# Float32r and bfloat16 products grouped within each accumulation of a two-layer decoder trunk

## The chip, the cores and the metric

The kernel runs on one core of one Trainium2 chip. The metric is the device time of one execution in microseconds. Three timed runs of the kernel before gave 1263.82, 1265.33 and 1266.68 us; the median is 1265.33.

## What is computed

A trunk of two layers over 1024 tokens of width 1024, with 256 memory tokens, everything in float32 (`x`, `mem` and all weights):

```python
for layer in range(2):
    h = x @ w_in[layer]                         # 1024 -> 3072: main | mem q | main gate | mem gate
    if layer == 0:  y_main = causal_pool(u_main)        # windows 2, 4, 8, 16 by group of 256 channels, then a 256 x 256 map
    else:           y_main = forgetting_attention(u_main, k, v, cum)   # 16 heads of 64, causal
    y_mem = memory_attention(q_mem, mem, w_mem_kv[layer])              # 4 heads of 128
    y = concat(y_main * silu(g_main), y_mem * silu(g_mem)) @ w_out[layer]      # 1536 -> 1024
    x = layer_norm(sqrt(2) * x + y)
# ahead of layer 1: k, v, forget logits = x @ w_kv_shared; cum = cumsum(log_sigmoid(logits))
# forgetting attention: softmax(q.k / 8 + cum[t] - cum[s]) @ v
```

## The kernel before

**Precision by three products.** Each float32 operand is split in two: `hi` is its float32r rounding, and a pair `lo` of bfloat16 tiles holds `lo[0]`, the remainder, and `lo[1]`, the operand itself in bfloat16. `three(a, b)` (line 184) gives for one contraction tile of 128 the three products that are summed in a PSUM bank: large `(ah, bh)` in float32r, and two small ones in bfloat16:

```python
return (ah, bh), (al[1], bl[0]), (al[0], bl[1])
```

The trace shows float32r operands as f32. The first operand is the stationary one, loaded ahead of each product by a load instruction (PEld in the profile); the second streams, mostly 512 columns. `hi_lo` (line 155) makes the split: ScalarE the `hi` (line 158), VectorE `lo[0]` (159), GpSimd `lo[1]` (160). In the forgetting attention `gp_hi_lo` (162) does all three on GpSimd for weights (163 to 165). Weights come through `split_w` (167): one DMA of 128 x 512 to a `raw` buffer (four of them), then `hi` and the `lo` pair in one buffer each of the tag `w` (six).

**Slabs.** Most of the work on TensorE is done in slabs (`slab`, line 194): 128 output channels for all 1024 tokens. A slab has two weight pieces of four contraction tiles. It allocates two PSUM banks (tag `pj`, three banks), one for each 512 tokens, and goes: for each piece, for each half of the tokens, for each of four contraction tiles, the three products (line 205), 48 in all. After the last product of a half, `evac` empties its bank: for gates a tanh on ScalarE (line 218) and a product on VectorE (219), else copies. A slab is a generator that yields after each product.

**Other sums.** `project` in `mem_kv` (line 231) sums 24 products of 256 columns for keys and values of the memory; `mm3` (189) sums a list of products, for the map of pooled channels (line 556), the logits and values of the memory attention (317, 342) and of the forgetting attention (756, 803), all seen at line 192; `v_first` (620) makes the first values and the forget logits with 272 columns (line 635); `OutProj.products` (403) does the output projection by chunks (`c`) of 512 of the 1536 inputs and 256 tokens, four banks, three chunks in turn 2, 0, 1 (line 411). After the third chunk `norm` (450) empties the banks on VectorE (459, 460), normalizes (462 to 472) and stores; in layer 0 TensorE then transposes the result (281) for layer 1.

**Order.** In layer 0's pooling and in the output projections a scheduler orders all engines. In the memory attention and the whole forgetting attention TensorE's order is written out by hand (`manual_schedule`), the other engines' is the scheduler's. There `Fill` (42) doles out the products of slabs between attention steps, by columns.

**Forgetting attention.** Per head and block of 128 queries, from the last block down (`probs`, line 737): GpSimd masks 128 columns of the row tile R (`affine_select`, 749); for each part of up to 512 keys two products make the logits (756), the large and small halves of q and k lying in the partitions, the second of them on bfloat16 views of the float32r tiles, read at every second element (`upper`, 94); VectorE adds R, takes the minimum and writes them (757); ScalarE takes exponentials (765) and f16 halves (786, VectorE 787), DMAs transpose them, and TensorE multiplies by the values (803).

**Start.** Nine products of 512 columns on zeros (line 92) stand ahead of the first weights.

## Time and profile before

| | |
|---|---|
| median of three runs | 1265.33 us (1263.82 to 1266.68) |
| profiled execution | 1265.82 us |
| its span, first to last instruction | 1263.9 us |
| TensorE matmuls / weight loads | 7018 of each |
| VectorE / ScalarE / GpSimd busy | 839.4 / 576.9 / 472.7 us |
| granted TensorE clock, mean | 0.996 |

The profile is one execution recorded by the hardware. PE is TensorE's matmuls, PEld its weight loads, DVE VectorE, ACT ScalarE, POOL GpSimd. In a row of groups stand line, engine, operation, tiles written and read (buffer numbers left out), shapes, the count, busy microseconds and mean nanoseconds, then the idle time of the engine just before such instructions and what ended it. In a row of a timeline stand start and length in microseconds, and the idle time before it in brackets. The durations of matmuls overlap and their ends are modelled, so how fast they follow each other is read from starts. By stages, 0 to 250 us are pooling group 0 and memory attention of layer 0, to 345 us the other groups, to 485 us the output projection, then memory attention and first projections of layer 1, from 682 to 1122 us the forgetting attention, then the last output projection.

### The profile page before, as it was taken

How to read it: one execution, taken by the hardware profiler on the slowest of the kernel's cores; microseconds unless marked ns; L12 is line 12 of the kernel's file. 1: busy time of each engine (PE TensorE's matmuls, PEld its weight loads, DVE VectorE, ACT ScalarE, POOL GpSimd, SP SyncE). 2: the span in 40 equal slices, each digit the busy share in tenths (PEclk: the TensorE clock that was granted, in tenths of full speed). 3: DMA queues.
4: the chain of work that ended last, by engine and by line, in shares of the span. 5: the costliest groups of instructions: out<-in, count | busy, mean ns of one | idle time of the engine just before them, and what ended most of it. 6: DMA issues, size and time to landing. Idle time of an engine off the chain costs nothing. (4 is left out here: it accounts for less than half of the span.)

```text
span 1263.9 us, 20169 instructions
## 1 busy us (share of the span) xinstructions
PE 1233.3 (98%) x7018; PEld 649.5 (51%) x7018; DVE 839.4 (66%) x1901; ACT 576.9 (46%) x1273; POOL 472.7 (37%) x582
## 2 busy tenths in 40 slices
PE   8999999999999999999999999999999999999997
PEld 3455664444444445556574555555555555554443
DVE  7544767385754467357735888877877788785644
ACT  4333653232321123356324777667766777762110
POOL 7444113252342234331303443444435334684110
PEclk9999999999999999999999999999999999999999
DMA  5233544232263324234525677868786889895430
GB/s 217 87 112 94 135 109 142 84 109 90 95 215 117 117 93 133 76 102 108 177 48 156 146 178 168 193 150 176 157 196 161 178 177 213 217 229 184 168 115 34
DMA packets 267414, 178.68 MB, mean 141 GB/s; under 512 B 212272, under 2 KB 225712, under 8 KB 267312
## 3 DMA queue, kind: packets, MB, share of 16 engines
q1 hardware_dynamic: 267312, 177.40, 53.3%
q8 instruction: 55, 0.90, 0.3%
q14 instruction: 47, 0.39, 0.1%
HBM read 94.97 MB, written 22.61 MB: 93 GB/s over the span
## 5 line engine op out<-in xcount | busy, mean ns | idle before, releaser
L205 PE MATMUL pj<-A,w 128*128 128x512 bf16 (+1 forms) x2928 | 728.2, 447 | 7.0 <-DVE Y L219 2.8
L205 PEld LDWEIGHTS pj<-A,w 128*128 128x128 f32 x976 | 188.0, 193 | 100.9 <-issue 4.0
L205 PEld LDWEIGHTS <-w 128*128 128x128 bf16 x1984 | 119.9, 98 | 231.5 <-issue 218.6
L160 POOL TENSOR_SCALAR w<-w 128x512 bf16<-128x512 f32 x106 | 110.3, 1041 | 263.1 <-ACT w L158 202.9
L159 DVE TENSOR_TENSOR w<-raw,w 128x512 bf16<-128x512 f32 x106 | 81.3, 768 | 93.6 <-ACT w L158 92.5
L765 ACT ACTIVATE T<-MK,s 128x512 f32<-128x512 f32 x192 | 110.8, 577 | 55.9 <-DVE s L757 43.3
L158 ACT CAST w<-raw 128x512 fp32r<-128x512 f32 x106 | 65.5, 618 | 150.0 <-PE pj L205 68.2
L787 DVE SCALAR_TENSOR_TENSOR P<-T,s,P 128x512 f16<-128x512 f32 x192 | 111.7, 612 | 32.7 <-ACT P L786 30.6
L160 POOL TENSOR_SCALAR T<-T 128x1024 bf16<-128x1024 f32 (+1 forms) x39 | 69.7, 1793 | 155.6 <-PE L L411 61.6
L192 PE MATMUL L<-B,B 128*128 128x512 f32 (+7 forms) x384 | 116.5, 429 | 9.5 <-DVE s L757 9.2
L786 ACT ACTIVATE P<-T,s 128x512 f16<-128x512 f32 x192 | 102.7, 576 | 47.7 <-ACT T L765 18.0
L749 POOL TENSOR_SCALAR_AFFINE_SELECT R<-R 128x128 f32<-128x128 f32 x128 | 41.3, 328 | 147.2 <-DVE s L757 125.8
L411 PEld LDWEIGHTS <-T 128*128 128x128 bf16 x736 | 42.9, 98 | 93.6 <-issue 92.4
L757 DVE CUSTOM_DVE_ANT_0 MK<-L,R 128x512 f32<-128x512 f32 (+3 forms) x128 | 72.8, 569 | 6.2 <-PE L L192 2.3
L192 PE MATMUL O<-T,V 128*128 128x128 f16 x1152 | 75.5, 220 | 0.8 <-DVE G L813 0.4
L192 PEld LDWEIGHTS <-V 128*128 128x128 f16 x1152 | 67.0, 98 | 14.6 <-issue 11.1
L159 DVE TENSOR_TENSOR T<-T,T 128x1024 bf16<-128x1024 f32 x23 | 31.3, 1361 | 63.5 <-PE L L411 42.9
L164 POOL TENSOR_TENSOR w<-raw,w 128x512 bf16<-128x512 f32 x54 | 69.1, 1279 | 4.8 <-PE pj L205 4.8
L158 ACT CAST T<-T 128x1024 fp32r<-128x1024 f32 x23 | 24.1, 1047 | 94.2 <-DMA T<-y0d 47.3
L163 POOL TENSOR_SCALAR w<-raw 128x512 fp32r<-128x512 f32 x54 | 33.6, 622 | 75.9 <-PE pj L205 75.6
L192 PEld LDWEIGHTS L<-B,B 128*128 128x128 f32 x192 | 37.1, 193 | 32.0 <-DVE s L757 18.1
L238 PE MATMUL pj<-T,w 128*128 128x256 bf16 (+1 forms) x384 | 49.2, 309 | 1.5 <-DVE w L159 1.0
(234 smaller groups left out, 1769.5 us busy)
## 6 DMA issues: line engine op xcount, KB each, us to landing
raw<-in_win_dram SPq DMA_DIRECT2D x96, 256.0 KB, 2.8
raw<-in_wout_dram SPq DMA_DIRECT2D x40, 256.0 KB, 2.8
B<-B SPq DMA_DIRECT2D x32, 256.0 KB, 3.9
R<-cumd SPq DMA_DIRECT2D x16, 512.0 KB, 4.6
y0d<-Y SPq DMA_DIRECT2D x12, 512.0 KB, 2.9
T<-y0d SPq DMA_DIRECT2D x12, 512.0 KB, 3.8
T<-y1d SPq DMA_DIRECT2D x11, 512.0 KB, 4.2
raw<-in_wmk_dram SPq DMA_DIRECT2D x16, 256.0 KB, 2.6
```

Source lines behind the costliest of these rows:

```text
L158: pin(nc.scalar.copy(hi, src))
L159: pin(nc.vector.tensor_tensor(lo[0], src, hi.bitcast(F32), ALU.subtract))
L160: nc.gpsimd.tensor_scalar(lo[1], hi.bitcast(F32), 1.0, 1.0, ALU.mult, ALU.mult)
L164: nc.gpsimd.tensor_tensor(lo[0], src, hi.bitcast(F32), ALU.subtract)
L192: nc.tensor.matmul(acc, a, b, start=i == 0, stop=i == len(terms) - 1)
L205: nc.tensor.matmul(accs[n], a, b, start=kt == 0 and i == 0, stop=kt == KT - 1 and i == 2,)
L238: nc.tensor.matmul(acc, w, m, start=pc == 0 and k == 0 and i == 0, stop=pc == 1 and k == 3 and i == 2,)
L411: nc.tensor.matmul(accs[a][nh], y, w, start=kt == 8 and i == 0, stop=kt == 7 and i == 2,)
L757: nc.vector.tensor_tensor_reduce(p[:, lo:up], lg, R[:, lo:up], 1.0, top, ALU.add, ALU.min, m[:, n : n + 1])
L765: nc.scalar.activation(e, p[:, lo:up], AF.Exp, bias=top, scale=-1.0, accum_out=sums[:, n, hd % 2, i : i + 1],)
L786: nc.scalar.activation(pair[:, lo:up], e, AF.Copy, scale=r)
L787: nc.vector.scalar_tensor_tensor(pair[:, L + lo : L + up], e, r, pair[:, lo:up], ALU.mult, ALU.subtract)
```

## The change

Within each accumulation all large (float32r) products stand together and all small (bfloat16) ones together. `grouped` puts the large first, or, `turned`, the small first; the turn alternates from bank to bank, so that equal kinds meet where two sums follow each other. A slab whose weights aren't given ready splits both pieces at its start and finishes 512 tokens, with a bank of their own, before the other 512. The two slabs with ready weights at the start alternate between the two banks product by product. In the output projection the groups reach over the four banks of a chunk: 16 large, 32 small, turned in chunk 0. In the forgetting attention the second product of the logits takes the float32r tiles themselves, and `upper` goes. The warm-up has three products as before, then four float32r and four bfloat16 ones on half the rows, on two banks.

```diff
@@ -88,12 +88,15 @@
     warm = pool.tile([P, NH], BF16, tag="w", name="warm", bufs=6)
     nc.vector.memset(warm, 0.0)
     idle = psum.tile([P, NH], F32, tag="O", name="idle", bufs=1)
-    for _ in range(9):
+    calm = pool.tile([P, NH], F32R, tag="w", name="calm", bufs=6)
+    nc.gpsimd.memset(calm.bitcast(F32), 0.0)
+    aside = psum.tile([P, NH], F32, tag="T", name="aside", bufs=2)
+    for _ in range(3):
         nc.tensor.matmul(idle, warm[:, :P], warm, start=True, stop=True)
-
-    def upper(hi):
-
-        return hi.bitcast(BF16)[..., 1::2]
+    for zeros in (calm, warm):
+        for _ in range(2):
+            for rows, bank in ((slice(0, 64), idle), (slice(64, P), aside)):
+                nc.tensor.matmul(bank, zeros[rows, :P], zeros[rows, :], start=True, stop=True)
 
     def nm(tag):
         count[0] += 1
@@ -186,6 +189,12 @@
         (ah, al), (bh, bl) = a, b
         return (ah, bh), (al[1], bl[0]), (al[0], bl[1])
 
+    def grouped(triples, turned=False):
+
+
+        large, small_ = [t[0] for t in triples], [m for t in triples for m in t[1:]]
+        return small_ + large if turned else large + small_
+
     def mm3(acc, terms):
 
         for i, (a, b) in enumerate(terms):
@@ -193,23 +202,40 @@
 
     def slab(pieces_dram, XH, XL, evac, banks=("pj", 3)):
 
-        accs = [ps([P, NH], *banks) for _ in range(2)]
-        for pc in range(2):
-            ready = isinstance(pieces_dram, list)
-            h, l = pieces_dram[pc] if ready else split_w(pieces_dram[pc], [P, 4, P])
+        ready = isinstance(pieces_dram, list)
+        ws = pieces_dram if ready else [split_w(p, [P, 4, P]) for p in (pieces_dram[0], pieces_dram[1])]
+
+        def terms(n, kts):
+            cols = slice(n * NH, (n + 1) * NH)
+            out = []
+            for kt in kts:
+                h, l = ws[kt // 4]
+                out.append(three((h[:, kt % 4, :], cut(l, slice(None), kt % 4)), (XH[:, kt, cols], cut(XL, slice(None), kt, cols))))
+            return out
+
+        def put(acc, a, b, start, stop):
+            nc.tensor.matmul(acc, a, b, start=start, stop=stop)
+            since[0] += NH
+
+        if ready:
+            accs = [ps([P, NH], *banks) for _ in range(2)]
+            for kt in range(KT):
+                both = [terms(n, [kt])[0] for n in range(2)]
+                for i in range(3):
+                    for n in range(2):
+                        put(accs[n], *both[n][i], kt == 0 and i == 0, kt == KT - 1 and i == 2)
+                        yield NH
             for n in range(2):
-                for k in range(4):
-                    kt = pc * 4 + k
-                    cols = slice(n * NH, (n + 1) * NH)
-                    for i, (a, b) in enumerate(three((h[:, k, :], cut(l, slice(None), k)), (XH[:, kt, cols], cut(XL, slice(None), kt, cols)))):
-                        nc.tensor.matmul(
-                            accs[n], a, b,
-                            start=kt == 0 and i == 0, stop=kt == KT - 1 and i == 2,
-                        )
-                        if kt == KT - 1 and i == 2:
-                            evac(slice(n * NH, (n + 1) * NH), accs[n])
-                        since[0] += NH
-                        yield NH
+                evac(slice(n * NH, (n + 1) * NH), accs[n])
+            return
+        for n in range(2):
+            acc = ps([P, NH], *banks)
+            order = grouped(terms(n, range(KT)), n == 1)
+            for j, (a, b) in enumerate(order):
+                put(acc, a, b, j == 0, j == len(order) - 1)
+                if j == len(order) - 1:
+                    evac(slice(n * NH, (n + 1) * NH), acc)
+                yield NH
 
     SLAB = 48 * NH
 
@@ -228,17 +254,19 @@
             hi_lo(mh[q // 2][:, two, :], cut(ml[q // 2], slice(None), two), r)
         kh, kl = halved(MK, [P, MH, NMEM])
 
+        turned = [False]
+
         def project(w_dram):
 
             acc = ps([P, NH], "pj", 3)[:, :NMEM]
+            terms = []
             for pc in range(2):
                 a, b = split_w(w_dram[pc], [P, 4, P])
-                for k in range(4):
-                    for i, (w, m) in enumerate(three((a[:, k, :], cut(b, slice(None), k)), (mh[pc][:, k, :], cut(ml[pc], slice(None), k)))):
-                        nc.tensor.matmul(
-                            acc, w, m,
-                            start=pc == 0 and k == 0 and i == 0, stop=pc == 1 and k == 3 and i == 2,
-                        )
+                terms += [
+                    three((a[:, k, :], cut(b, slice(None), k)), (mh[pc][:, k, :], cut(ml[pc], slice(None), k))) for k in range(4)
+                ]
+            turned[0] = not turned[0]
+            mm3(acc, grouped(terms, turned[0]))
             return acc
 
         two, v = (MK([P, MH, 2 * 2, P], F16) for _ in range(2))
@@ -314,7 +342,7 @@
                     h = 2 * hp + j
                     at = slice(None), slice(i * P, (i + 1) * P)
                     qh, ql = qs[h][0][at], cut(qs[h][1], *at)
-                    mm3(lg[:, j, :], three((qh, ql), (kh[:, h, :], cut(kl, slice(None), h))))
+                    mm3(lg[:, j, :], grouped([three((qh, ql), (kh[:, h, :], cut(kl, slice(None), h)))], j == 1))
                 pair = slice(2 * hp, 2 * hp + 2)
                 nc.vector.tensor_reduce(m[:, pair], lg, AX.X, ALU.max, negate=True)
                 nc.vector.tensor_scalar(ms[:, pair], m[:, pair], MSCALE, None, ALU.mult)
@@ -401,18 +429,19 @@
             return accs[:2], accs[2:]
 
         def products(self, accs, c, yh, yl):
+            terms = []
             for a in range(2):
+                rows = slice(a * P, (a + 1) * P)
                 for nh in range(2):
                     for k in range(4):
                         kt = 4 * c + k
-                        wh, wl = (w[kt % 2] for w in self.ws[nh][kt // 2])
-                        rows = slice(a * P, (a + 1) * P)
-                        for i, (y, w) in enumerate(three((yh[:, k, rows], cut(yl, slice(None), k, rows)), (wh, wl))):
-                            nc.tensor.matmul(
-                                accs[a][nh], y, w,
-                                start=kt == 8 and i == 0, stop=kt == 7 and i == 2,
-                            )
-                            yield NH
+                        w = tuple(part[kt % 2] for part in self.ws[nh][kt // 2])
+                        terms.append([(accs[a][nh], x) for x in three((yh[:, k, rows], cut(yl, slice(None), k, rows)), w)])
+            order = grouped(terms, c == 0)
+            firsts, lasts = ({id(acc): j for j, (acc, _) in way} for way in (reversed(list(enumerate(order))), enumerate(order)))
+            for j, (acc, (y, w)) in enumerate(order):
+                nc.tensor.matmul(acc, y, w, start=c == 2 and j == firsts[id(acc)], stop=c == 1 and j == lasts[id(acc)])
+                yield NH
 
         def early(self, y, yh, yl):
 
@@ -552,8 +581,8 @@
                         a, b = wh[at], cut(wl, *at)
                         at = slice(None), slice(n * NH, (n + 1) * NH)
                         ph, pl = pms[ct][0][at], cut(pms[ct][1], *at)
-                        terms += three((a, b), (ph, pl))
-                    mm3(acc, terms)
+                        terms.append(three((a, b), (ph, pl)))
+                    mm3(acc, grouped(terms, n == 1))
                     yn = ys[d][:, n * NH : (n + 1) * NH]
                     nc.vector.scalar_tensor_tensor(yn, acc, pschalf[:, f : f + 1], yn, ALU.mult, ALU.mult)
                 nc.sync.dma_start(y0d[f // 4, :, f % 4, :], ys[d])
@@ -627,13 +656,13 @@
                 hi_lo(wh[kt // 4][:, kt % 4, :], cut(wl[kt // 4], slice(None), kt % 4), r)
             for s in range(ST):
                 acc = ps([P, NH], "pj", 3)
+                terms = []
                 for kt in range(KT):
                     at = slice(None), kt, slice(s * P, (s + 1) * P)
-                    a, b = XH[at], cut(XL, *at)
-                    h, l = wh[kt // 4][:, kt % 4, :], cut(wl[kt // 4], slice(None), kt % 4)
-                    for i, (u, w) in enumerate(three((a, b), (h, l))):
-                        nc.tensor.matmul(acc[:, :FW], u, w, start=kt == 0 and i == 0, stop=kt == KT - 1 and i == 2)
-                        yield FW
+                    terms.append(three((XH[at], cut(XL, *at)), (wh[kt // 4][:, kt % 4, :], cut(wl[kt // 4], slice(None), kt % 4))))
+                for j, (u, w) in enumerate(grouped(terms, s % 2 == 1)):
+                    nc.tensor.matmul(acc[:, :FW], u, w, start=j == 0, stop=j == 3 * KT - 1)
+                    yield FW
                 nc.scalar.copy(toks[s // 4][:, s % 4, :], acc[:, : 2 * P])
                 nc.vector.tensor_tensor(flog[:, s * HEADS : (s + 1) * HEADS], acc[:, 2 * P : FW], bfb, ALU.add)
 
@@ -753,7 +782,7 @@
             parts = [(0, L)] if L <= NH else [(0, 384), (384, L)] if L == 640 else [(0, NH), (NH, L)]
             for n, (lo, up) in enumerate(parts):
                 lg = ps([P, NH], "L", 2)[:, : up - lo]
-                mm3(lg, ((q[:, qs], kx[:, lo:up]), (upper(q[:, qs]), upper(ky[:, lo:up]))))
+                mm3(lg, ((q[:, qs], kx[:, lo:up]), (q[:, qs], ky[:, lo:up])))
                 nc.vector.tensor_tensor_reduce(p[:, lo:up], lg, R[:, lo:up], 1.0, top, ALU.add, ALU.min, m[:, n : n + 1])
                 top = m[:, n : n + 1]
                 if n == 0:

```

## The prediction

> **What bounds the kernel now.** I read the page's busy times first, then TensorE's groups by form, then narrow stretches of its timeline, and last what it waits for.
>
> ```profile
> span 1263.9 us, 20169 instructions
> PE 1233.3 (98%) x7018; PEld 649.5 (51%) x7018; DVE 839.4 (66%) x1901; ACT 576.9 (46%) x1273; POOL 472.7 (37%) x582
> L205 PE MATMUL pj<-A,w 128*128 128x512 bf16 x1952 | 599.2, 385 | 2.5 <-POOL A L160 2.1 <-DVE A L159 0.4
> L205 PE MATMUL pj<-A,w 128*128 128x512 f32 x976 | 557.3, 571 | 4.4 <-DVE Y L219 2.8 <-ACT A L158 1.6
> L205 PE MATMUL pj<-A,w x2928: 376/390/988, 4.9 to 1121.2; 128*128 128x512 f32 x194, 128*128 128x512 bf16 x2
> ```
>
> TensorE is busy for 98% of the span, so the time is what its matmuls cost one after another, and a change of their order counts only if it changes their spacing. Busy times overlap (matmuls are pipelined), so I take spacings from starts. A weight load starts when the matmul ahead of it begins to stream:
>
> ```profile
> 610.18 0.19 PEld L205 LDWEIGHTS pj<-A,w 128*128 128x128 f32 x1
> 610.63 0.12 PEld L205 LDWEIGHTS <-w 128*128 128x128 bf16 x2 [0.26 <-issue]
> 610.86 0.19 PEld L205 LDWEIGHTS pj<-A,w 128*128 128x128 f32 x1
> ```
>
> One triple (f32, bf16, bf16) takes 610.86 - 610.18 = 0.68 us. The first bf16 takes 610.63 to 610.86, 0.23 us. From the f32 load to the first bf16 are 0.45 us, of which one bf16 stream lies ahead of the f32 product. What that bf16 costs is seen where bf16 follows other 16-bit products:
>
> ```profile
> 602.45 0.84 PE L192 MATMUL O<-T,MK 128*128 128x128 f16 x12
> 603.14 1.06 PE L205 MATMUL pj<-A,w 128*128 128x512 bf16 x4
> 603.35 0.19 PEld L205 LDWEIGHTS pj<-A,w 128*128 128x128 f32 x1
> L205 PE MATMUL pj<-A,w 128*128 128x512 bf16 x1 | 0.4, 379 | 0.0
> ```
>
> The bf16 at 603.14, behind f16, is followed by the second at 603.35: 0.216 us (unrounded), and its own record lasts 379 ns (last row, that one alone). A bf16 behind f32 has the median record, 390 ns; the group's mean of 385 is half of each. So **the first 16-bit product behind an f32 one costs 11 ns more** (0.227 against 0.216). The f32 product costs 0.45 - 0.216 = 0.234. Sum of a triple: 0.234 + 0.227 + 0.216 = 0.677, as seen.
>
> Would f32 behind f32 be cheaper? The start of the kernel has three in a row:
>
> ```profile
> 17.15 0.19 PEld L205 LDWEIGHTS L<-A,w 128*128 128x128 f32 x1
> 17.37 0.42 PEld L205 LDWEIGHTS pj<-A,w 128*128 128x128 f32 x2
> 18.06 0.11 PEld L205 LDWEIGHTS <-w 128*128 128x128 bf16 x2 [0.27 <-issue]
> ```
>
> The first of them streams from 17.37 (there the next load starts), the bf16 follows at 18.06: 0.69 us for three, 0.23 each. An f32 product costs the same in a run as alone; only the 16-bit product behind it gains.
>
> **The change part by part.**
>
> *Grouping.* Counted in the order of the built programs, an f32 product is followed by a 16-bit one 1848 times before (slabs 933, output projections 384, line 192's sums 338, line 238's 129, line 635's 64) and 302 times after (slabs 180, all short sums 96, output projections 20, six others). 1546 x 0.011 = **-17.0 us**. At 256 columns the extra is the same 10 to 11 ns. A scheduler that pulled the groups apart would show in that count; it doesn't.
>
> *f32 behind short products.* Longer f32 runs are cut by f16 products more often: f16 directly before f32 occurs 13 times before and 44 after.
>
> ```profile
> 164.43 0.55 PEld L192 LDWEIGHTS <-MK 128*128 128x128 f16 x9
> 164.93 0.19 PEld L205 LDWEIGHTS pj<-A,w 128*128 128x128 f32 x1
> 165.27 0.12 PEld L205 LDWEIGHTS <-w 128*128 128x128 bf16 x2 [0.15 <-issue]
> ```
>
> From f32 load to bf16 are 0.35 us with only an f16 stream (0.056) ahead: 0.294 instead of 0.234, since 0.056 us does not cover the load. 31 x 0.06 = **+1.9 us**.
>
> *Forgetting attention: q by ky as float32r.* 192 bf16 products at stride 2 become f32.
>
> ```profile
> L192 PE MATMUL L<-B,B 128*128 128x512 f32 x80 | 43.9, 571 | 7.0 <-DVE s L757 6.8
> L192 PE MATMUL L<-B,B 128*128 128x512 bf16 x80 | 32.1, 401 | 0.0
> ```
>
> The bf16 one has 401 ns where others have 390, so it costs 0.227 to 0.238, the f32 one 0.234: between -0.004 and +0.007 each, -0.8 to +1.3 us. The 16 of 128 columns come to f32 behind f32 of 128, which lays the second load bare by about 0.05 each (as above): 0.8. I take **+1.2 us**.
>
> *Slabs by 512 tokens.* A bank is now allocated per half slab. With three banks in turn, a bank comes back after two half slabs of other work, 10.6 us; before, in half of the cases, after one, 5.3 us. This wait was of that kind:
>
> ```profile
> 278.59 0.68 DVE L219 SCALAR_TENSOR_TENSOR Y<-Y,pj 128x512 f32<-128x512 f32 x1
> 279.32 2.59 PE L205 MATMUL pj<-A,w 128*128 128x512 f32 x7 [1.99 <-DVE Y L219]
> PE pj L205 <- DVE Y L219: 2.8, 2, 2.0
> ```
>
> VectorE came late by 2.0 us to the gate that frees the bank; 5.3 us more would cover it. **-2.8 us** (bounds -2.8 and 0).
>
> The same edit holds both weight pieces of a slab to its end. Six "w" buffers are three pieces. From the last product that reads a buffer to the first that reads its next content, TensorE has 4.5 us of products in the typical slab after (2.4 at the least outside the start), against 3.0 to 6.9 before; in the forgetting attention 5.6 us against 12 or more.
>
> ```profile
> L158 ACT CAST w<-raw 128x512 fp32r<-128x512 f32 x106 | 65.5, 618 | 150.0 <-PE pj L205 68.2
> L159 DVE TENSOR_TENSOR w<-raw,w 128x512 bf16<-128x512 f32 x106 | 81.3, 768 | 93.6 <-ACT w L158 92.5
> L160 POOL TENSOR_SCALAR w<-w 128x512 bf16<-128x512 f32 x106 | 110.3, 1041 | 263.1 <-ACT w L158 202.9
> L163 POOL TENSOR_SCALAR w<-raw 128x512 fp32r<-128x512 f32 x54 | 33.6, 622 | 75.9 <-PE pj L205 75.6
> L164 POOL TENSOR_TENSOR w<-raw,w 128x512 bf16<-128x512 f32 x54 | 69.1, 1279 | 4.8 <-PE pj L205 4.8
> ```
>
> The large half, needed first, takes 0.62 us; the small ones (0.77, 1.04) are needed eight products later. With 2.4 us or more this stays hidden: **0**. On GpSimd it is 0.62 + 1.28 + some 0.65 per piece, hidden by 5.6 us as long as GpSimd is free; if not, see the rivals.
>
> *Ends of the layers.* In the output projection all large products of four banks come first, so banks finish 8 small products apart (1.73 us) instead of 12 (2.7 us). The first row's second bank then finishes 3.46 us before the last product, not 5.4, and VectorE's norm follows:
>
> ```profile
> 1253.38 1.71 PE L411 MATMUL L<-B,T 128*128 128x512 f32 x6
> 1249.69 0.69 DVE L459 SCALAR_TENSOR_TENSOR G<-G,pj 128x512 f32<-128x512 f32 x1 [1.29 <-PE pj L411]
> 1255.66 0.68 DVE L459 SCALAR_TENSOR_TENSOR G<-G,L 128x512 f32<-128x512 f32 x1
> 1257.10 0.21 DVE L462 BATCH_NORM_AGGREGATE s<-s 128x2 f32<-128x12 f32 x1
> ```
>
> TensorE ends at 1255.09. VectorE works from 1249.69 to 1257.10 without a pause, 7.4 us; begun 3.46 us before the end it comes to the last row's aggregate 3.9 us after it, where it is now 2.0: **+1.9 us**. At the end of layer 0 the same norm feeds the next projections:
>
> ```profile
> 487.17 1.70 PE L238 MATMUL pj<-T,w 128*128 128x256 bf16 x13 [0.54 <-DVE s L463]
> 489.87 1.45 PE L238 MATMUL pj<-T,w 128*128 128x256 bf16 x11 [1.00 <-DVE w L159]
> ```
>
> TensorE already waits 1.5 us there, and two weight pieces now have under 1 us of products ahead of them: **+1.5 us** (0 to 4).
>
> *The forgetting attention's VectorE.*
>
> ```profile
> 682.00:1122.00 440.00, 430.23 (x2782) 234.42 (x2781) 350.67 (x1012) 311.59 (x734) 194.55 (x317) 1.00 0.81 179
> PE L L192 <- DVE s L757: 9.2, 15, 2.0
> ```
>
> VectorE is at 80% there and holds TensorE up for 9.2 us. Some 28 slabs of 16 triples save 28 x 16 x 0.011 = 4.9 us in it; a fifth, its share of tight heads as I guess it, comes back as waiting: **+1.0 us** (0 to 4.9). The warm-up has 11 products instead of 9 and ends before 7.3 us, when the second slice of x is there: 0.
>
> Sum: -17.0 + 1.9 + 1.2 - 2.8 + 1.5 + 1.9 + 1.0 = -12.3. The profiled execution took 1265.8, 0.5 above the median of the three runs, 1265.3; so 1253.5 on its own scale and **1253.0 us** against the median. About 0.2% (2.5 us) is what a measurement of this kernel can tell from no change.
>
> **The rivals.**
>
> *A: f32 products speed up too.* Had every f32 product in a run the spacing of bf16, 0.216 for 0.234, another 1546 x 0.018 = 28 us would go: 1225 us. The three at 17.37 to 18.06 speak against it, 0.23 each, but a run of three is short. [...]
>
> *B, slower: GpSimd's queue.* GpSimd waits for weight buffers at L163 (75.6 us in 37 waits above), and behind that wait in its queue stand the masks of the forgetting attention, for which VectorE's L757 waits, and TensorE for that.
>
> ```profile
> L749 POOL TENSOR_SCALAR_AFFINE_SELECT R<-R 128x128 f32<-128x128 f32 x128 | 41.3, 328 | 147.2 <-DVE s L757 125.8
> ```
>
> Buffers now come free at the end of a slab, up to 7 us later. If each of the 27 slabs split on GpSimd puts one L164 (1.28 us) in front of a mask that is due, that is 27 x 1.28 = 35 us: 1288 us. It decides once GpSimd has more than 5.6 - 2.55 = 3 us of work queued at a release. GpSimd busy for 194.55 of 440 us and masks of 0.33 us speak against it.
>
> *C: the gain is given back.* All small prices at their upper ends: -17.0 + 1.9 + 1.3 + 0.8 + 0 + 4 + 2.6 + 4.9 = -1.5: 1264 us. The last 2.6 is the tail if VectorE's rows also drift apart.
>
> **How the numbers follow.** Forecast 0.66, A 0.07, B 0.13, C 0.14. The forecast's own range: if runs of f32 differ by 2 ns per product, that is 1546 x 0.002 = 3 us either way; the boundary, the bank wait and VectorE add +2.5, +2.8, +3.9 upward, and TensorE's other waits, were half to go, 5 us downward: 1243 to 1262. With C and a part of what lies below, 1240 to 1266 leaves out 2 in 10. Faster by over 0.2%: forecast, A and a third of C, 0.77; same 0.06; slower B and the rest of C, 0.17.
>
> **What would show it.** The mean bf16 record at the slabs' line falls from 385 to about 380, f32 stays near 571, and a run of f32 loads stands 0.23 us apart (0.216 would be A). The bank wait on the gate's VectorE line is gone. TensorE's last product lies some 14 us earlier, and about 10.7 us, not 8.8, before the end. B would show as waits of TensorE for VectorE's maxima well over 9.2 us with VectorE waiting for the masks. The forecast is wrong if loads of f32 in runs of eight or sixteen stand further apart than 0.24 us: each 0.01 there costs 15 us.

## The result, and the profile after the change

| kernel | median us (range, runs) | ratio to before, 95% interval |
|---|---|---|
| before | 1264.57 (1260.49 to 1266.68, 6) | |
| after | 1255.45 (1253.28 to 1259.6, 6) | 0.9938 [0.9912, 0.9963] |

The change is 9.1 us faster; the forecast was 1253.0, 12.3 us faster. The profiled execution of after is the longest of its six, 1259.6 us, some 4 us over the median, so its waits are a little larger than usual. The page of after, first line and busy times:

```profile
span 1257.9 us, 20137 instructions
...
PE 1208.1 (96%) x6910; PEld 766.9 (61%) x7020; DVE 839.7 (67%) x1901; ACT 578.5 (46%) x1273; POOL 468.7 (37%) x583
```

TensorE's busy time fell by 25 us (from 1233.3), the span by only 6.0. Some 6 of the 25 are no saving: 110 of the 7020 products, all of them bfloat16, have no record in this trace and leave small gaps. Their weight loads are all there, and the spacings and the sum below are read from these. Still, the new order saved much more than was forecast, and most of the difference came back as time in which TensorE stands idle. Its groups by form (count, busy us, mean ns of one, idle before it) show where:

```profile
L217 PE MATMUL pj<-A,w 128*128 128x512 bf16 x1869 | 448.7, 382 | 11.2 <-POOL w L163 4.1 <-POOL A L163 2.1 <-DVE A L162 0.8
L217 PE MATMUL pj<-A,w 128*128 128x512 f32 x976 | 266.8, 409 | 1.5 <-ACT A L161 1.3 <-POOL w L166 0.2
```

The bfloat16 mean is 382 ns (385 before; 380 was forecast). The idle time ahead of these products is 11.2 us, where it was 2.5; some 4 of it are the gaps of missing records, the rest are the waits named in the row. Do not read the float32r mean of 409 (571 before) as a saving of 162 ns: that is how far the records of neighbours overlap. Spacings come from the starts of the weight loads: in the trace of before a load starts in the median 2 ns after a bfloat16 product ahead of it begins, 11 ns if that one stands behind float32r. The load of a bfloat16 product behind a float32r one doesn't start so early, but 4 ns before its own product, so the forecast's sentence on when a load starts doesn't hold for it. A slab of after, and then the same stretch of before (start, duration, what is loaded, count):

```profile
42.74 3.61 PEld L217 LDWEIGHTS pj<-A,w 128*128 128x128 f32 x16
46.62 6.59 PEld L217 LDWEIGHTS <-w 128*128 128x128 bf16 x32 [0.26 <-issue]
53.33 1.79 PEld L217 LDWEIGHTS pj<-A,w 128*128 128x128 f32 x8
```

```profile
42.72 0.19 PEld L205 LDWEIGHTS pj<-A,w 128*128 128x128 f32 x1
...
53.58 0.19 PEld L205 LDWEIGHTS pj<-A,w 128*128 128x128 f32 x1
```

From the first float32r load to the one that begins the next round, 16 triples (48 products) take 10.86 us before and 10.59 after: 0.27 less. The switches account for 15 x 0.011 = 0.165 of it. The other 0.105 is float32r in a run: 16 loads in 3.61 us, the last of them lasting 0.19, are (3.61 - 0.19) / 15 = **0.228 us** apart, against the 0.234 of one that stands alone. That is what the forecast missed.

TensorE's waits in after (what for; us in total, times, longest):

```profile
PE L L201 <- DVE s L786: 10.3, 17, 3.8
PE pj L217 <- POOL w L163: 4.1, 2, 2.5
PE pj L201 <- DVE w L162: 2.7, 1, 2.7
```

The wait for the gate that frees a bank (2.8 us at VectorE's L219 before) is gone, as forecast. In its place stand 4.1 us for the low half of a weight piece, split on GpSimd (L163). At the same place of the program, in the first layer's projections:

```profile
272.14 0.81 PE L217 MATMUL pj<-A,w 128*128 128x512 bf16 x3
272.31 2.08 POOL L163 TENSOR_SCALAR T<-T 128x1024 bf16<-128x1024 f32 x1 [1.85 <-ACT T L161]
273.41 1.52 DVE L162 TENSOR_TENSOR w<-raw,w 128x512 bf16<-128x512 f32 x1
274.36 1.04 POOL L163 TENSOR_SCALAR w<-w 128x512 bf16<-128x512 f32 x1
275.46 1.03 PE L217 MATMUL pj<-A,w 128*128 128x512 bf16 x2 [2.51 <-POOL w L163]
```

(Rows of TensorE, GpSimd and VectorE, in order of time.) TensorE's small products need all of the slab's low halves early, and the one split on GpSimd stands behind the 2.08 us split of another tile. When it is ready, TensorE has stood for 2.51 us. But GpSimd is late by little: VectorE's half of the same weights is ready at 274.93, only 0.47 us before GpSimd's at 275.40 (at the second such place, near 326 us, it is again 0.47). What follows adds to the wait. Four windows of after (PE busy and count first after the length; the column ahead of the DMA share is the granted clock, in parts of full speed):

```profile
272.00:275.40 3.40, 0.90 (x4) 0.22 (x3) 3.40 (x4) 1.86 (x4) 3.09 (x3) 1.00 0.51 154
275.50:278.90 3.40, 3.40 (x9) 1.20 (x10) 2.04 (x3) 0.00 (x0) 1.50 (x2) 0.50 0.60 172
483.70:487.00 3.30, 0.53 (x4) 0.10 (x1) 3.30 (x9) 1.60 (x4) 2.12 (x4) 1.00 0.19 70
487.10:490.50 3.40, 3.40 (x17) 2.70 (x18) 2.47 (x4) 0.62 (x1) 0.00 (x0) 0.50 0.66 231
```

Each of these two stalls is followed by 3.4 us at a granted clock of 0.50, in which bfloat16 products of 512 columns stand 0.427 us apart instead of 0.216 (the loads from 275.5 us), those of 256 columns 0.213 instead of 0.109 (from 487.1 us): 1.7 us more. After has four such stretches ahead of its end (from 275.5, 487.1, 664.6 and 681.7 us), before has two (280.2, 877.6): 2 x 1.7 = 3.4 us. They are no fixed price of a stall: e2, e5 and e6 below have the same stall near 275 us (2.5, 2.4 and 2.5 us) and keep the full clock behind it; e10 has the stretch too.

The first row of the waits, for VectorE's maxima, has its longest wait (3.8 us) where the forgetting attention begins, and there VectorE itself waits:

```profile
680.71 0.69 DVE L786 CUSTOM_DVE_ANT_0 MK<-L,R 128x512 f32<-128x512 f32 x1 [3.10 <-DMA R<-cumd]
681.46 1.94 PE L201 MATMUL L<-B,B 128*128 128x512 f32 x4 [3.81 <-DVE s L786]
```

The DMA of the row tile R comes late. Before, VectorE waited 1.59 us for it, and TensorE 2.04 us.

The tail of after, VectorE's rows behind TensorE's last product:

```profile
1246.50 1.03 PE L443 MATMUL L<-B,T 128*128 128x512 bf16 x4
...
1249.28 0.69 DVE L489 BATCH_NORM_STATS2 s<-G 128x6 f32<-128x512 f32 x1
...
1251.07 0.20 DVE L491 BATCH_NORM_AGGREGATE s<-s 128x2 f32<-128x12 f32 x1
```

TensorE ends at 1247.53 and the last aggregate comes at 1251.27, 3.74 us later (3.9 was forecast, 2.0 before).

**The sum.** I added up TensorE's paces, as the starts in these two traces show them, over the order of the built programs: 216 ns for 512 columns of a 16-bit product (109 for 256, 56 for 128), 11 more behind float32r, 18 more for float32r alone and 12 more in a run (234 and 228 at 512 columns), 60 more where a float16 product of 128 columns (56 ns) does not cover its load (190 ns), and 5.5 for bfloat16 at stride 2 (an estimate, the middle of the forecast's 0 to 11). What the starts of the loads show above that is waiting, half-clock stretches included.

| | before | after | difference | forecast |
|---|---|---|---|---|
| TensorE's work | 1206.7 | 1183.5 | -23.2 | -13.9 |
| its waiting, first to last product | 40.7 | 56.9 | +16.2 | -0.3 |
| last load to the end | 9.4 | 10.9 | +1.5 | +1.9 |
| first product starts | 4.9 | 5.7 | +0.8 | 0 |

The other -1.3 us of the 6.0 lie between the first product and the second: the second load comes 2.2 us later than the pace before, 0.9 us after. The run-to-run spread of such sums is not known, since there is one trace of each kernel, and that of after is of its longest run. The forecast column puts its terms -17.0, +1.9 and +1.2 in the first row and -2.8, +1.5 and +1.0 in the second.

### The profile page after: what moved, and what is told of

It is laid out like the page before. It is cut to its first block, busy times and chain, and to the rows that moved or that the text cites. A ratio compares the mean times of both kernels' runs of the same rounds, so it can differ in the third digit from the quotient of the medians.

```text
span 1257.9 us, 20137 instructions
## 1 busy us (share of the span) xinstructions
PE 1208.1 (96%) x6910; PEld 766.9 (61%) x7020; DVE 839.7 (67%) x1901; ACT 578.5 (46%) x1273; POOL 468.7 (37%) x583
## 5 line engine op out<-in xcount | busy, mean ns | idle before, releaser
L217 PE MATMUL pj<-A,w 128*128 128x512 bf16 (+1 forms) x2845 | 691.5, 391 | 12.7 <-POOL w L163 4.1
L217 PEld LDWEIGHTS <-w 128*128 128x128 bf16 x1984 | 180.4, 98 | 223.7 <-issue 36.8
L217 PEld LDWEIGHTS pj<-A,w 128*128 128x128 f32 x976 | 178.5, 189 | 40.7 <-ACT A L161 2.9
L163 POOL TENSOR_SCALAR w<-w 128x512 bf16<-128x512 f32 x106 | 102.1, 967 | 224.0 <-PE pj L217 104.5
L162 DVE TENSOR_TENSOR w<-raw,w 128x512 bf16<-128x512 f32 x106 | 87.7, 833 | 70.9 <-PE pj L217 49.7
L163 POOL TENSOR_SCALAR T<-T 128x1024 bf16<-128x1024 f32 (+1 forms) x39 | 67.1, 1725 | 170.0 <-ACT T L161 58.8
L443 PEld LDWEIGHTS <-T 128*128 128x128 bf16 x736 | 70.9, 98 | 86.7 <-issue 3.2
L201 PE MATMUL L<-B,B 128*128 128x512 f32 (+3 forms) x384 | 109.5, 388 | 10.7 <-DVE s L786 10.3
L201 PEld LDWEIGHTS L<-B,B 128*128 128x128 f32 x384 | 70.1, 189 | 39.8 <-DVE s L786 22.9
L786 DVE CUSTOM_DVE_ANT_0 MK<-L,R 128x512 f32<-128x512 f32 (+3 forms) x128 | 72.7, 568 | 10.9 <-PE L L201 3.6
L201 PEld LDWEIGHTS <-V 128*128 128x128 f16 x1152 | 67.7, 98 | 19.7 <-issue 8.1
L201 PE MATMUL O<-T,V 128*128 128x128 f16 x1152 | 75.0, 219 | 3.1 <-DVE G L842 1.9
L201 PE MATMUL pj<-T,w 128*128 128x256 bf16 (+1 forms) x384 | 47.1, 283 | 2.8 <-DVE w L162 2.7
L443 PE MATMUL pj<-B,T 128*128 128x512 bf16 (+1 forms) x181 | 48.0, 392 | 0.7 <-POOL T L163 0.5
```

What stands on the lines that cost most here:

```text
L162: pin(nc.vector.tensor_tensor(lo[0], src, hi.bitcast(F32), ALU.subtract))
L163: nc.gpsimd.tensor_scalar(lo[1], hi.bitcast(F32), 1.0, 1.0, ALU.mult, ALU.mult)
L201: nc.tensor.matmul(acc, a, b, start=i == 0, stop=i == len(terms) - 1)
L217: nc.tensor.matmul(acc, a, b, start=start, stop=stop)
L443: nc.tensor.matmul(acc, y, w, start=c == 2 and j == firsts[id(acc)], stop=c == 1 and j == lasts[id(acc)])
L786: nc.vector.tensor_tensor_reduce(p[:, lo:up], lg, R[:, lo:up], 1.0, top, ALU.add, ALU.min, m[:, n : n + 1])
```

## Experiments

My theory behind the first runs: the grouping saves more than forecast, and it is the places where the new order bunches things (both weight pieces at once in the slabs, four banks finishing together in the output projection) that take it back. The rival: the waits are the usual answer to a faster TensorE, whatever the order. Each kernel was measured beside the kernel before on the same chip; between chips (e1 to e4, e5 to e8, e9 and e10 share one each) the ratios compare better than the times (before took 1264.72, 1265.15 and 1266.56 us on these three).

| kernel | median us (range) | ratio to before, 95% interval |
|---|---|---|
| after | 1255.45 (1253.28 to 1259.6) | 0.9938 [0.9912, 0.9963] |
| e1_piece | 1256.03 (1253.61 to 1256.48) | 0.9926 [0.9913, 0.9938] |
| e2_rows | 1252.79 (1252.11 to 1254.75) | 0.9907 [0.9893, 0.992] |
| e3_both | 1252.42 (1251.57 to 1255.54) | 0.9899 [0.9884, 0.9914] |
| e4_tokens | 1264.28 (1261.59 to 1266.99) | 0.9993 [0.9982, 1.0003] |
| e5_fox | 1259.39 (1257.63 to 1260.68) | 0.9957 [0.9941, 0.9973] |
| e6_warm | 1257.26 (1255.14 to 1258.51) | 0.994 [0.9923, 0.9957] |
| e7_dve | 1266.56 (one run) | |
| e8_tokpiece | **1247.82** (1246.99 to 1249.36) | **0.9868 [0.9849, 0.9886]** |
| e9_twos | 1253.28 (1252.49 to 1256.9) | 0.9896 [0.9877, 0.9914] |
| e10_dve | 1264.66 (one run) | |

**e1_piece: the slab's old order by weight pieces, grouped.** Both banks of a slab are open again, groups have 12 products.

```diff
-        for n in range(2):
-            acc = ps([P, NH], *banks)
-            order = grouped(terms(n, range(KT)), n == 1)
+        accs = [ps([P, NH], *banks) for _ in range(2)]
+        for pc in range(2):
+            ws.append(split_w(pieces_dram[pc], [P, 4, P]))
+            for n in range(2):
+                order = grouped(terms(n, range(4 * pc, 4 * pc + 4)), n == 1)
...
```

> The changed kernel, but a slab goes again by weight pieces: piece 0 for both halves of the tokens, then piece 1, both banks open, the twelve products of a piece and half grouped (4 large, 8 small, the second half turned). In the order of the program f32 is followed by a 16-bit product 326 times (302 in the changed kernel), so the gain from grouping is the same within 0.5 us. Theory (waits come from holding both pieces to the slab's end): TensorE's waits for GpSimd's split (4.1 us, near 272 and 324 us) and some of the waits at the start of the forgetting attention go, and the time is 2 to 5 us under the changed kernel, about 1251. Rival (TensorE is simply faster than what VectorE and the DMAs feed it with): the waits move elsewhere and the time stays within 1.5 us of the changed kernel, 1254 to 1257. Second rival (the free bank at half a slab matters): the wait of TensorE for the gate's VectorE line of 2 us comes back and the time is 2 us longer.

Measured 1256.03 us, no different from after. TensorE's waits:

```profile
PE L L201 <- DVE s L788: 10.8, 19, 0.9
PE pj L217 <- DVE Y L247: 3.5, 2, 2.5
PE pj L201 <- DVE w L162: 2.8, 1, 2.8
```

The wait for GpSimd's half is gone, so the slab's new order caused it; and the gate's bank wait is back (3.5 us), with a half-clock stretch behind it from 276.4 us. The two orders of the slab exchange one stall for another of the same size.

**e2_rows: the output projection grouped by row.** Two banks, not four, share a group, so that the first row's banks finish early.

```diff
-            terms = []
+            order = []
             for a in range(2):
                 rows = slice(a * P, (a + 1) * P)
+                terms = []
...
-            order = grouped(terms, c == 0)
+                order += grouped(terms, a == 1)
```

> The changed kernel, but in the output projection the products are grouped row by row (128 tokens: 8 large and 16 small over two banks, the second row turned), not over all four banks of a chunk. f32 followed by 16 bit: 313 times instead of 302. Theory (grouping over four banks makes the banks finish bunched at the end of a chunk, and the norm on VectorE comes late): layer 0's output projection takes 134.5 us instead of 137.5, the tail behind TensorE's last product shrinks from about 10.5 to about 9 us, and the time is 3 to 5 us under the changed kernel. Rival (the waits in the output projection come from VectorE's work as such): the same time within 1 us.

Measured 1252.79, 2.7 us below after by the medians, 3.9 by the ratios (the intervals overlap a little). Its tail, TensorE's last products and VectorE behind them:

```profile
1240.65 0.62 PE L444 MATMUL L<-B,T 128*128 128x512 f32 x2
...
1242.26 1.28 DVE L490 BATCH_NORM_STATS2 s<-G 128x6 f32<-128x512 f32 x2
1243.57 0.21 DVE L492 BATCH_NORM_AGGREGATE s<-s 128x2 f32<-128x12 f32 x1
```

The last aggregate comes 1243.78 - 1241.27 = 2.51 us behind TensorE's last product, not 3.74: 1.2 us. The output projection of layer 0 takes 135.5 us from its first load to its last, not 137.5 (136.4 for 137.7 to the load that follows it), and the wait at the layers' boundary is halved:

```profile
PE pj L201 <- DVE w L162: 1.4, 1, 1.4
```

**e3_both: e1 and e2 together.**

> Both edits together: slabs by weight pieces and the output projection grouped by rows. Theory: the two gains add, 1246 to 1249 us; this would be faster than both kernels. Rival: the time stays above 1253, because VectorE in the forgetting attention takes the difference.

1252.42, as e2 alone and in neither of the expected ranges: the slab by pieces adds nothing to it.

**e4_tokens: slabs by 512 tokens, nothing grouped.** Made from the kernel before; the triples stay as they were.

```diff
...
+        ws = [split_w(p, [P, 4, P]) for p in (pieces_dram[0], pieces_dram[1])]
+        for n in range(2):
+            acc = ps([P, NH], *banks)
+            cols = slice(n * NH, (n + 1) * NH)
+            for kt in range(KT):
+                h, l = ws[kt // 4]
+                for i, (a, b) in enumerate(three(...)):
...
```

> The kernel before, with one part of the change: slabs by 512 tokens with both weight pieces split at the start and one bank per half; the triples stay as they were (f32 followed by 16 bit 1848 times, as before). Theory (the new slab order costs waits): 0 to 4 us longer than the kernel before, with waits of TensorE for GpSimd's split near 273 us. Rival (its later bank reuse helps, as the prediction had it): 2.8 us shorter, 1261 to 1262, the wait for the gate's VectorE line gone and none in its place.

1264.28, ratio 0.9993: the order of the tokens by itself is worth nothing that can be told. Its waits:

```profile
PE L L192 <- DVE s L770: 4.9, 8, 2.2
PE pj L205 <- POOL A L160: 2.0, 5, 0.5
...
PE pj L192 <- DVE Y L232: 1.0, 1, 1.0
```

No product of a slab waits for a gate, nor for GpSimd's half, since an ungrouped slab needs the second piece only in its second quarter. The stage with the old gate wait (from the end of layer 0's memory values to its output projection) is 3.4 us shorter in its trace (150.8 for 154.2). Of this 1.7 us are the half-clock stretch from 280.2 us, which is in the trace of before alone, and 1.8 the gate's bank wait, which went from 2.8 to the 1.0 of the last row and moved to a product of the pooled map (L192). In the medians nothing is left of it, and which wait took it is not shown.

**e5_fox: the logits' second product as bfloat16 at stride 2 again.**

```diff
-                mm3(lg, ((q[:, qs], kx[:, lo:up]), (q[:, qs], ky[:, lo:up])))
+                mm3(lg, ((q[:, qs], kx[:, lo:up]), (upper(q[:, qs]), upper(ky[:, lo:up]))))
```

> The changed kernel, but in the forgetting attention the second product of the logits reads the bfloat16 views at every second element again, as before. f32 followed by 16 bit: 403 times instead of 302, and 1546 instead of 1839 f32 products stand in runs. Theory (as predicted, f32 here costs 1.2 us in all, and grouping gains 11 ns per switch avoided): 101 more switches cost 1.1 us, the bfloat16 products save 1.2 or a little less: within 1 us of the changed kernel. Rival (bfloat16 at stride 2 is dearer than its record says, or f32 in runs is cheaper): 2 us or more longer than the changed kernel.

1259.39, 3.9 us above after by the medians and 2.4 by the ratios; the two intervals overlap, so it is shown only that float32r is not dearer here. The paces say the same: for a pair of 512 columns ahead of float32r of 384, the median distance from its first load to that next load is 448 ns in after and 455 in e5 (16 pairs each). Groups of e5 by form:

```profile
L205 PE MATMUL L<-B,B 128*128 128x512 f32 x80 | 40.6, 530 | 7.0 <-DVE s L790 7.0
...
L205 PE MATMUL L<-B,B 128*128 128x512 bf16 x80 | 32.3, 404 | 0.0
```

The bfloat16 product at stride 2 has 404 ns, where one behind float32r elsewhere has the median record of 390: the upper end of the forecast's bounds for it was nearer the truth, and the float32r product in its place is one that stands in a run.

**e6_warm: the old warm-up of nine bfloat16 products.** The new one is taken out, the rest stays.

```diff
...
-    for _ in range(3):
+    for _ in range(9):
         nc.tensor.matmul(idle, warm[:, :P], warm, start=True, stop=True)
-    for zeros in (calm, warm):
...
```

> The changed kernel with the old warm-up of nine bfloat16 products. Theory (the start is limited by the loads of x and their splits): the first product of a slab comes at 4.9 us instead of 5.7, the clock is full later (10.6 us instead of 5.9), and the time agrees with the changed kernel within 1 us. Rival (the earlier full clock counts): 1.5 to 2.5 us longer, half of the 4.7 us by which the full clock comes later.

1257.26, ratio 0.994 as after: no difference. TensorE's start in e6, then in after:

```profile
1.25 4.02 PE L92 MATMUL idle<-warm 128*128 128x512 bf16 x9 [1.25 <-DVE warm L89]
5.07 0.55 PE L210 MATMUL pj<-A,w 128*128 128x512 f32 x1
6.59 0.51 PE L210 MATMUL pj<-A,w 128*128 128x512 f32 x1 [0.97 <-ACT A L154]
```

```profile
5.10 0.63 PE L99 MATMUL idle<-warm 64*128 64x512 bf16 x1
5.66 0.57 PE L217 MATMUL pj<-A,w 128*128 128x512 f32 x1
6.77 0.50 PE L217 MATMUL pj<-A,w 128*128 128x512 f32 x1 [0.54 <-ACT A L161]
```

The first product comes 0.6 us later in after, the second, which waits for the slice of x, within 0.2 us: the data decides, as forecast. What an earlier full clock is worth e6 does not tell. The clock that was expected at 10.6 us is full from 5.2 us in its trace, and from 5.9 in after; with the new warm-up it is full from 10.2 to 10.5 us in e1, e2 and e5. So the warm-up alone does not set it.

**e7_dve and e10_dve: more work for VectorE in the forgetting attention.** Two reductions more per block; e7 reads a constant, e10 the block's own logits.

```diff
+            for _ in range(2):
+                nc.vector.tensor_reduce(edge[:, :1], ident, AX.X, ALU.max)
```

```diff
+            for _ in range(2):
+                nc.vector.tensor_reduce(edge[:, :1], p[:, :P], AX.X, ALU.max)
```

> The changed kernel with two more reductions on VectorE (128 columns of a constant, the result unused) per block of the forgetting attention, 256 in all, about 0.2 us each, some 50 us of VectorE time there on top of its 352 of 440 us. Theory (in the forgetting attention VectorE already holds TensorE up, and that is where part of TensorE's saving went): the forgetting attention gets more than 10 us longer and TensorE's wait for VectorE's maxima grows from 10 to over 20 us. Rival (TensorE alone is the bound there and VectorE has room): less than 3 us longer.

e7 answers another question than its own. The group's row (duration min/median/max, first and last start):

```profile
L792 DVE TENSOR_REDUCE edge<-ident x256: 270/286/291, 10.0 to 162.8; 128x1 f32<-128x128 f32 x128
```

The reductions depend on nothing in their block, and so were put between 10.0 and 162.8 us, long before the forgetting attention. Inconclusive.

> The changed kernel with two further reductions on VectorE over each block of the forgetting attention's own logits, 256 in all; they change nothing that is computed, and stand where their block stands. At some 0.28 us each they add about 72 us to a VectorE that is busy for 352 of the stage's 440 us. If VectorE sets what the forgetting attention gives back (as the prediction had it), the stage gets longer by more than 10 us and the wait of the logits' products for the additions on VectorE grows from 10 to over 20 us. If TensorE's own order and the banks set it, and VectorE has room, the stage gets longer by less than 3 us.

With its own logits as input the work stays in place. The stretch of the forgetting attention in e10 and in after (VectorE's busy time is the third), and e10's wait:

```profile
682.00:1122.00 440.00, 425.32 (x2753) 281.78 (x2798) 394.47 (x1254) 311.08 (x732) 191.09 (x314) 1.00 0.80 177
```

```profile
682.00:1122.00 440.00, 429.35 (x2775) 285.48 (x2821) 352.13 (x1016) 314.78 (x740) 197.19 (x320) 1.00 0.79 180
```

```profile
PE L L201 <- DVE s L786: 14.4, 21, 3.0
```

VectorE goes from 80% to 90%: 42 us more of busy time in this window (the 256 records add up to 71 us, but overlap). From the first load of the logits to the last the stage takes 441.9 us for 438.0, the wait goes from 10.3 to 14.4, and the run, 1264.66, is 5.1 above the profiled one of after, of which the slower chip has some 2 (before took 1266.56 us there and 1264.57 beside after). Neither expectation is clearly met, for these are single traces: e2 and e6, whose forgetting attention is that of after, have 435.8 and 439.3 us there. So 42 us of work cost 3 to 6 us, about a tenth. VectorE does hold TensorE up by a little, and is not what the stage's time is made of.

**e8_tokpiece: the version that the first runs point to.** From e2: slabs by 512 tokens, but grouped within each weight piece, so that the second piece is needed half a bank later.

```diff
-            order = grouped(terms(n, range(KT)), n == 1)
+            order = grouped(terms(n, range(4))) + grouped(terms(n, range(4, KT)), True)
```

> The changed kernel with the output projection grouped by rows (as in the run before) and in slabs the halves of the tokens one after the other as in the changed kernel, but grouped piece by piece: 4 large, 8 small of piece 0, then 8 small, 4 large of piece 1. So a bank comes back late and piece 0 is free at three quarters of the slab. f32 followed by 16 bit: 337 times. Theory (both the wait for GpSimd's split and the wait for the gate come from the order of a slab): both waits near 272 and 325 us are gone, 4 us less than the run with rows alone, 1248 to 1249. Rival (the waits there belong to VectorE's pooling work, and something else comes late): 1251 to 1253.

1247.82, faster than both kernels: its interval lies wholly below that of after and of e2. Its waits:

```profile
PE L L201 <- DVE s L787: 9.3, 13, 4.5
PE T L309 <- DVE G L502: 3.5, 5, 1.0
...
PE pj L217 <- DVE w L162: 1.7, 1, 1.7
```

No slab waits for GpSimd's half or the gate's bank any more. At the place of after's first stall 1.7 us are left of 2.5: the wait for VectorE's half of the same weights (the last row), which GpSimd's had hidden. The gate's bank holds a product of the pooled map for 1.1 us (L201, on L245). Ahead of the end the clock is halved once, from 675.0 us, for 6.83 us, two lengths of the stretches above, behind the 4.5 us wait where the forgetting attention begins. Around the place of after's stall it stays full:

```profile
272.00:275.40 3.40, 1.73 (x9) 0.65 (x8) 3.40 (x4) 1.71 (x4) 3.40 (x3) 1.00 0.52 154
275.50:278.90 3.40, 3.40 (x16) 2.11 (x15) 2.34 (x4) 0.24 (x1) 1.61 (x2) 1.00 0.81 225
```

Work 1182.8 and waiting 48.3, by the sum above: nearly 9 of the 16 us are back, with the work as low as in after. (The two profiled runs are 10.2 us apart, the medians 7.6, so some of the 9 is the choice of run.)

**e9_twos: is it the grouping, and by how much?** From e8, with the slabs' triples merely turned one against the other, so that float32r products stand in twos.

```diff
-            order = grouped(terms(n, range(4))) + grouped(terms(n, range(4, KT)), True)
+            order = [m for kt in range(KT) for m in grouped(terms(n, [kt]), kt % 2 == 1)]
```

> The version with slabs by tokens and the output projection by rows, but in the slabs the three products of each contraction tile merely stand turned, L S S | S S L, so that the float32r products stand in twos and not in runs of four. By the order of the instructions it has 648 changes from float32r to a 16-bit product against 337, and 1492 float32r products behind another float32r one against 1803. If grouping pays by every change left out (11 ns each) and by every float32r product that stands behind another (some 6 ns each), it is 311 x 0.011 + 311 x 0.006 = 5.3 us longer than the version that it is made from: about 1253, a ratio of .991. If only the changes count, 3.4 us longer, 1251.3. If waits take up what a longer or shorter run of TensorE gives, it stays within 1.5 us of 1247.8.

1253.28, 5.5 us above e8 by the medians. But the chip is another one, and by the ratios it is 3.5 us, which is what was expected if only the switches count; the two intervals overlap. A slab of it, the first load of a pair and the one 16 triples later:

```profile
40.77 0.41 PEld L217 LDWEIGHTS pj<-A,w 128*128 128x128 f32 x2
...
51.52 0.41 PEld L217 LDWEIGHTS pj<-A,w 128*128 128x128 f32 x2
```

10.75 us for 16 triples: between 10.86 (alone) and 10.59 (grouped); e8 has 10.61. Of the 0.11 that twos save, 8 x 0.011 = 0.09 are the switches; the float32r product gains its 6 ns only in longer runs (by the starts, the first of a pair takes 0.231 us and the second 0.238, together no less than two alone). So the 5.3 us that were expected credited twos with a gain that they do not have: by the paces e9 loses 0.14 us per 16 triples to e8, up to 8 us over some 60 slabs. Measured are 3.5 to 5.5, so that waits may have taken up a part.

## Why the prediction was right, and by which of its steps

The sign and the size were right, but the size by two misses that pulled against each other: TensorE's work fell by 23 us, not 14, and its waiting grew by 16, not by nothing. That the two nearly cancel is luck.

- **Switches, -17.0: right.** The 11 ns stand in the starts of after, e8 and e9 too (227 ns behind float32r, 216 elsewhere). e9, with more switches, is slower, but cannot tell the switches from the runs.
- **"An f32 product costs the same in a run as alone": this step failed.** The three loads at the start gave 0.69 / 3 = 0.23, and 0.23 against 0.234 was taken for equal. The true 0.228 is 6 ns less, and 1847 float32r products stand behind another float32r one in after, 105 in before: 1742 x 0.006 = 10.5 us (an estimate: it lets products of fewer columns gain as much). The forecast's own range allowed 2 ns. The rival A (0.216) had a third of its way: 6 of 18 ns. The loads of after stand 0.216 us apart for bfloat16 alone.
- **float32r behind short products, +1.9: not measured by itself;** the 60 ns stand in the sum above.
- **q by ky as float32r, +1.2: wrong in sign, as far as e5 tells.** The pair is 7 ns cheaper, not up to 7 dearer.
- **The gate's bank wait, -2.8: right,** gone in after; in e4 1.0 of it is left at another product.
- **Weights held, 0: failed.** The step looked at when buffers come free and at how long the splits take, and not at what else stands in GpSimd's queue: a 2.08 us split stood in front, and VectorE's half came late too. That is 4.1 us of waits, and in this trace a half-clock stretch of 1.7. e1 takes it away by undoing the slab's order, e8 takes away 2.4 of the 4.1 by asking for the second piece later. It is rival B's mechanism, at another place and about a ninth of its price: it struck twice in the first layer's projections, and not in the forgetting attention, where the wait for maxima went only from 9.2 to 10.3.
- **Boundary, +1.5: too low.** That stage's waiting grew by 3.3 us (3.3 to 6.6): the waits at its start went from 1.5 us (1.0 for the weights' low half) to 2.7, all for that half, and a half-clock stretch follows. e6, with the same code and no such stretch, waits 5.0. e2 brings it back to 4.4.
- **Tail, +1.9: right** (+1.5), and e2 shows its cause, the four banks in one group: 1.2 of it goes.
- **VectorE in the forgetting attention, +1.0: too low, and its reason only in part right.** That stage's work fell by 5.0 us and its waiting grew by 3.2. e10 shows that VectorE passes on only about a tenth of added work, so it isn't a plain limit there. 1.8 of the 3.2 lie at the stage's first wait, which the DMA of R ends, and no more than that is shown: the stage's length in e2, after and e6, where its code is the same, spreads over 3.5 us. What else holds TensorE there stays open: with the same slab order e4 waits 14.7 us in it and e8 21.4, and no run here separates the banks of the logits from the order of the heads.
- **Not foreseen: some waits here cost more than their length.** Half-clock stretches were in the trace of before (280.2 and 877.6 us), and the prediction did not look for what begins them. Two more are 3.4 us of the 16 in the trace of after; e1 and e6 have two like before, so the change alone does not set their number. And the out-projection of layer 0 waits 3.3 us more (4.4 to 7.7), of which e2 takes back 1.5.

What would show it: the bank wait's end and the distance of TensorE's last product from the end (10.4 us; 10.7 forecast) came as said. TensorE's last product lies 7.6 us earlier than before, not 14. The float32r records did not stay near 571 ns, and that told nothing, since they overlap.

## What to carry to other kernels

In accumulations of mixed types put equal types together, over the bank's edge too: here each float32r-to-bfloat16 switch left out was worth 11 ns and each float32r product in a longer run 6 more, and a difference that is met 1700 times has to be read to the nanosecond before it is called nothing. But group no further than operands and banks arrive: a group that needs all weights at once, or ends four banks together, takes back what it saves (grouping by weight piece and by row kept the saving and gave 1247.8 us). And look for the granted clock behind each stall of TensorE, since here a wait of 2.5 us cost 1.7 us more in some traces (after, e10) and not in others (e2, e5, e6).

## What the runs showed of the hardware

- A half-clock stretch lasts 3.41 us (once each in e5, e8 and e9 6.83, twice that), and those of after start on one grid: from 275.5 to 487.1, 664.6 and 681.7 us are 62, 114 and 119 times 3.413 us. The 3.40 us ahead of the first held 0.90 us of products; at the same place e8 held 1.73, and the clock stayed full. In e2 the 2.5 us stall near 275 us lies in two lengths of its grid, with 2.20 and 2.05 us of products, and the clock stays full. No plain threshold in the work ahead is shown: the 3.40 us ahead of 664.6 us held 1.97 us of short float32 products, and half rate followed. What begins such a stretch stays open.
- float32r products of 512 columns keep 0.234 us alone (before) and a median of 0.228 inside a run (after), where bfloat16 has 0.216 (the last before a bfloat16 one mostly 0.238, the median of 408 in e9).
